# A decoder trunk on one core: the SBUF pools opened in another order

## The chip, the cores and the metric

The kernel runs on one NeuronCore of a Trainium2 chip. The metric is the device time of one execution in microseconds (us). The engines are TensorE (PE in the profile, its weight loads PEld), VectorE (DVE), ScalarE (ACT), GpSimd (POOL) and SyncE (SP), which here issues nearly all transfers.

## The reference, cut to what matters

Two layers of a decoder trunk on 256 tokens of width 1024, float32, with three parallel mixers, a cross-attention into 256 memory tokens and a gated feed-forward:

```python
for l in range(DEPTH):                                   # DEPTH = 2
    h = rmsnorm(x, norm_mix[l])
    p = h @ w_in[l]                                      # 1024 -> 5888 columns
    a_x, a_c, a_b, q, k, v, g, z, gates = jnp.split(p, IN_SPLITS, axis=-1)
    y_a = short_conv_mixer(a_x, a_c, a_b, conv_w[l]) @ w_a_out[l]
    r = retention(rotary(q), rotary(k), v, ret_gn[l])
    y_b = (jax.nn.silu(g) * r) @ w_b_out[l]
    y_c = spatial_gating(jax.nn.gelu(z), sg_ln[l], sg_w[l], sg_b[l]) @ w_c_out[l]
    g_a, g_b, g_c = jnp.split(jax.nn.sigmoid(gates), 3, axis=-1)
    x = x + (g_a * y_a + g_b * y_b + g_c * y_c) @ w_o[l]
    h = rmsnorm(x, norm_xa[l]); mm = rmsnorm(mem, norm_mem[l])
    x = x + cross_attention(h, mm, xa_q[l], xa_k[l], xa_v[l], xa_o[l])
    h = rmsnorm(x, norm_ffn[l])
    x = x + (jax.nn.silu(h @ w1[l]) * (h @ w3[l])) @ w2[l]
return rmsnorm(x, final_norm)
```

## The kernel before, in words

**Weights.** All weight matrices lie in HBM as one stream in the order of use, in 320 tiles of 128 partitions x 1024 float32 (512 KB each). `fetch` (lines 92 to 109) loads the next tile into one of 5 `raw` buffers through SP's queue, ACT rounds it into one of 4 `hi` buffers (line 106), and DVE subtracts to give the rest in one of 4 `lo` buffers (recorded under line 67, the helper `tt`). `hi` and `lo` have the type float32r. `weights` (line 111) fetches one tile ahead of the matmuls.

**Activations** are kept as such a pair too: `xs` is the normed residual (split at lines 201 and 202), `mo`, `mg`, `qx`, `pt`, `ox` (tag "op"), `mmt` (tag "M"), `kT` and the first half of the feed-forward's hidden layer `aA` (tag "A"), `vt` and the second half `aB` (tag "B").

**Products.** Every product is the sum of three: high by high, high by rest, rest by high. All TensorE instructions are recorded under line 43, where `InOrder` issues them in the order of the code. There are three kinds of stream:

- `chunk_T` (f, gt, ax, ac, ab, q, k, wo, xo, w): for each half i of a chunk a pair of matmuls, one of 512 moving columns (both parts of the activation) on the `hi` weights, then one of 256 moving columns on the `lo` weights. Here a weight tile is the stationary operand, the activation the moving one.
- `chunk_N` and `chunk_pair` (qk, v, z, g, the first xv): the weight tile moves, 512 columns at a time, and the activation is stationary.
- `chunk_y`, the scores s, the weighted values av, the narrow xv and the last two chunks of w: 256 moving columns in every matmul.

**Order.** TensorE's order is that of the code. A scheduler in the building library sets the order of the other engines. SP's loads of a `raw` buffer wait until DVE has read what was in it before.

**Memory.** A pool takes its place in SBUF when it is opened: `const`, `res` (`xT`, `xs`), `wts` (`raw`, `hi`, `lo`), `wrk` (all else), from low addresses to high. Each partition holds the same layout. PSUM pools (`psm`, `pss`) are apart.

Of the kernel before, what the change touches and what calls it, by code (L numbers as in the profile page):

```python
# [54 lines left out]
def decoder_trunk(ctx: ExitStack, tc: tile.TileContext, a, out):  # L55
    nc = tc.nc
    V, A, G, T = nc.vector, nc.scalar, nc.gpsimd, InOrder(tc, nc.tensor)

    const = ctx.enter_context(tc.tile_pool(name="const", bufs=1))
    res = ctx.enter_context(tc.tile_pool(name="res", bufs=1))  # L60
    wts = ctx.enter_context(tc.tile_pool(name="wts", bufs=3))
    wrk = ctx.enter_context(tc.tile_pool(name="wrk", bufs=2))
    psm = ctx.enter_context(tc.tile_pool(name="psm", bufs=2, space=bass.MemoryType.PSUM))
    pss = ctx.enter_context(tc.tile_pool(name="pss", bufs=4, space=bass.MemoryType.PSUM))

# [665 lines left out]
```

## Time and profile before

| | |
|---|---|
| device time, median of 3 runs | 968.31 us (968.21 to 970.08) |
| the profiled execution, its own time | 969.4 us |
| its span, first to last instruction | 967.6 us, mean granted clock 0.995 |
| PE busy | 951.8 us, 98% of the span |
| DVE, ACT, POOL busy | 713.7, 539.8, 296.1 us |
| transfers | 175.53 MB, 181 GB/s mean |

The span is the time between the first and the last instruction of the trace. The chain of work that ended last is followed back from the last instruction, at each step to what released it; its pieces name an engine, the tile that is written and the number of instructions. From a piece of one stream its start-to-start spacing follows as length over count. The duration of one matmul in the trace is longer than that spacing, since matmuls are pipelined.

### The profile page before, as it was taken

To read this page: it belongs to the slowest core of one execution; us is meant where nothing else is said; L and a number is where in the kernel's file an instruction comes from. 1 tells how busy PE (TensorE), PEld (TensorE's weight loads), DVE (VectorE), ACT (ScalarE), POOL (GpSimd) and SP (SyncE) were. 2 spreads that over 40 slices of the span, in tenths; PEclk is the share of its full clock that TensorE was granted. 3 is DMA by queue.
4 is the path that set the end of the run, shared out by engine and by line. 5 is a ranking of instruction groups with operands and counts; after the bars stand their busy time and mean duration, and the time that the engine had idled before them with its cause. 6 is when DMAs were issued, how large, how long until landed. Compare 5 with 4: busy or idle time off the path is not lost.

```text
span 967.6 us, 14606 instructions
## 1 busy us (share of the span) xinstructions
PE 951.8 (98%) x5622; PEld 836.8 (86%) x5622; DVE 713.7 (74%) x884; ACT 539.8 (56%) x740; POOL 296.1 (31%) x232
## 2 busy tenths in 40 slices
PE   8999999999999999999999989999999999999996
PEld 6788889888998888888888878998889888888886
DVE  7679789886768866657655896799776778666654
ACT  6565765565645755654456465545665466656431
POOL 5943021320114644432134230024100345444211
PEclk9999999999999999999999999999999999999998
DMA  9664665555546565555656355555644556556541
GB/s 310 245 228 145 192 203 186 190 182 170 172 133 194 177 198 191 193 187 180 197 179 194 111 180 193 195 179 172 196 153 151 154 187 191 187 194 194 180 151 44
DMA packets 52630, 175.53 MB, mean 181 GB/s; under 512 B 6096, under 2 KB 6608, under 8 KB 52560
## 3 DMA queue, kind: packets, MB, share of 16 engines
q1 hardware_dynamic: 52128, 174.03, 55.9%
q8 instruction: 44, 0.72, 0.3%
q10 hardware_dynamic: 432, 0.57, 0.2%
q14 instruction: 26, 0.21, 0.1%
HBM read 173.53 MB, written 1.05 MB: 180 GB/s over the span
## 4 chain that ended last, share of the span: by engine, by line
PE 96%; DVE 2%; DMA 1%; issue 0%; SPq 0%; ACT 0%; DVEq 0%
PE f L43 25%; PE gt L43 14%; PE w L43 13%; PE y L43 5%; PE k L43 5%; PE xo L43 5%; PE wo L43 5%; PE xv L43 5%; PE q L43 5%; PE z L43 2%; PE g L43 2%; PE v L43 2%; PE qk L43 2%; PE av L43 1%; PE ac L43 1%; PE s L43 1%
## 5 line engine op out<-in xcount | busy, mean ns | idle before, releaser
L67 DVE TENSOR_TENSOR lo<-raw,hi 128x1024 fp32r<-128x1024 f32 (+1 forms) x321 | 436.8, 1363 | 200.0 <-ACT hi L106 198.0
L106 ACT ACTIVATE hi<-raw 128x1024 fp32r<-128x1024 f32 (+1 forms) x321 | 338.9, 1057 | 315.1 <-issue 67.5
L43 PE MATMUL f<-xs,hi 128*128 128x512 f32 x704 | 245.2, 393 | 0.0
L43 PE MATMUL f<-xs,lo 128*128 128x256 f32 x704 | 196.1, 279 | 0.0
L43 PEld LDWEIGHTS f<-xs,hi 128*128 128x128 f32 x704 | 131.9, 187 | 30.1 <-issue 0.4
L43 PE MATMUL gt<-xs,hi 128*128 128x512 f32 x384 | 136.5, 400 | 2.8 <-DVE ev L67 2.7
L43 PEld LDWEIGHTS f<-xs,lo 128*128 128x128 f32 x704 | 132.6, 188 | 0.0
L67 POOL TENSOR_TENSOR sq<-xT 128x512 f32<-128x512 f32 x27 | 45.8, 1695 | 239.3 <-DVE xT L67 234.5
L43 PE MATMUL gt<-xs,lo 128*128 128x256 f32 x384 | 107.8, 281 | 0.0
L67 POOL TENSOR_TENSOR ev<-ev,rb_ffn 128x512 f32<-128x512 f32 x44 | 63.8, 1453 | 108.3 <-DVE ev L67 85.3
L43 PEld LDWEIGHTS gt<-xs,hi 128*128 128x128 f32 x384 | 72.7, 189 | 20.6 <-DVE ev L67 4.0
L43 PEld LDWEIGHTS gt<-xs,lo 128*128 128x128 f32 x384 | 73.2, 191 | 0.0
L43 PE MATMUL w<-aB,hi 128*128 128x512 f32 (+1 forms) x198 | 62.7, 372 | 0.0
L43 PE MATMUL w<-aA,hi 128*128 128x512 f32 (+1 forms) x198 | 62.3, 371 | 0.0
L67 POOL TENSOR_TENSOR ev<-ev 128x256 f32<-128x256 f32 x44 | 50.5, 1151 | 20.1 <-ACT ev L597 20.1
L202 DVE SCALAR_TENSOR_TENSOR xs<-xT,par,xs 128x256 fp32r<-128x256 f32 x48 | 49.1, 1062 | 4.2 <-ACT xs L201 4.2
L43 PE MATMUL w<-aB,lo 128*128 128x256 f32 x176 | 49.5, 281 | 0.0
L43 PE MATMUL w<-aA,lo 128*128 128x256 f32 x176 | 49.4, 281 | 0.0
L43 PE MATMUL y<-mo,hi 128*128 128x256 f32 x256 | 46.1, 283 | 0.0
L43 PE MATMUL k<-mmt,hi 128*128 128x512 f32 x128 | 45.6, 400 | 0.0
L43 PE MATMUL q<-xs,hi 128*128 128x512 f32 x128 | 45.5, 398 | 0.0
L43 PE MATMUL xo<-ox,hi 128*128 128x512 f32 x128 | 45.4, 399 | 0.0
(251 smaller groups left out, 1779.9 us busy)
## 6 DMA issues: line engine op xcount, KB each, us to landing
raw<-in_ws SPq DMA_DIRECT2D x304, 512.0 KB, 3.5
raw<-in_ws SPq DMA_DIRECT2D x32, 256.0 KB, 4.0
m<-in_memT SPq DMA_DIRECT2D x12, 256.0 KB, 4.0
xT<-in_xT SPq DMA_DIRECT2D x4, 256.0 KB, 5.2
dec<-in_dec SPq DMA_DIRECT2D x1, 512.0 KB, 6.0
wm<-in_wsT SPq DMA_DIRECT2D x2, 256.0 KB, 4.8
out<-xT ACTq DMA_DIRECT2D x2, 256.0 KB, 2.3
sgg<-in_sgg SPq DMA_DIRECT2D x1, 256.0 KB, 5.1
```

The source lines that it names most:

```text
L43: ins = getattr(self.engine, name)(*args, **kwargs)
L67: e.tensor_tensor(o, x, y, op=op)
L106: A.activation(hi[:, sl], raw[:, sl], AF.Copy)
L202: V.scalar_tensor_tensor(lo, x, scale, f32(hi), ALU.mult, ALU.subtract)
```

## The change

The two pools `wrk` and `wts` are opened ahead of `const` and `res`. Since the first pool that is opened gets the lowest addresses, everything moves:

```diff
+    wrk = ctx.enter_context(tc.tile_pool(name="wrk", bufs=2))
+    wts = ctx.enter_context(tc.tile_pool(name="wts", bufs=3))
     const = ctx.enter_context(tc.tile_pool(name="const", bufs=1))
     res = ctx.enter_context(tc.tile_pool(name="res", bufs=1))
-    wts = ctx.enter_context(tc.tile_pool(name="wts", bufs=3))
-    wrk = ctx.enter_context(tc.tile_pool(name="wrk", bufs=2))
     psm = ctx.enter_context(tc.tile_pool(name="psm", bufs=2, space=bass.MemoryType.PSUM))
```

Every engine's instructions stand in the same order with the same waits in both programs: 5024 rows on PE, 817 on DVE, 727 on ACT, 209 on POOL, 362 on SP. What differs is where the tiles lie. In bytes from the start of a partition, as the two built programs have them, with the remainder of the start by 256 behind it:

| tiles | before | after |
|---|---|---|
| `xs` | 34880 (64) | 211264 (64) |
| `xT` | 26688 (64) | 203072 (64) |
| `raw`, 5 buffers | 51264 to 71744 (64) | 139648 to 160128 (128) |
| `hi`, 4 buffers | 71744 to 88128 (64) | 160128 to 176512 (128) |
| `lo`, 4 buffers | 88128 to 104512 (64) | 176512 to 192896 (128) |
| tag "B": `aB`, `vt`, mixb | 110656 (64) | 22656 (128) |
| tag "M": `mmt`, mixm | 133184 (64) | 45184 (128) |
| tag "op", 2 buffers | 149568, 165952 (64) | 61568, 77952 (128) |
| tag "A": `aA`, `kT`, gs | 198656 (0) | 110656 (64) |
| `ev`, 4 buffers | from 187808 (160) | from 99808 (224) |
| m2 and pp, 2 buffers | from 223232 (0) | from 135232 (64) |

The matmul operands start at these addresses plus multiples of 512 bytes.

## Rows read from the trace of the kernel before

**Rows 1.** The page: busy time by engine, then the chain's shares.
```profile
PE 951.8 (98%) x5622; PEld 836.8 (86%) x5622; DVE 713.7 (74%) x884; ACT 539.8 (56%) x740; POOL 296.1 (31%) x232
PE 96%; DVE 2%; DMA 1%; issue 0%; SPq 0%; ACT 0%; DVEq 0%
```

**Rows 2.** Pieces of the chain: start us, us, engine, tile, count.
```profile
44.05 10.89 PE g L43 x48
91.22 22.19 PE gt L43 x128
119.63 27.73 PE gt L43 x160
147.36 23.03 PE y L43 x192
176.04 22.62 PE wo L43 x128
216.07 14.13 PE q L43 x80
231.61 5.55 PE q L43 x32
258.32 2.88 PE xv L43 x24
314.41 105.39 PE f L43 x608
419.81 62.10 PE w L43 x352
790.38 105.39 PE f L43 x608
```

**Rows 3.** Matmuls by form: tiles, shapes, count | busy us, mean ns | idle before.
```profile
L43 PE MATMUL f<-xs,hi 128*128 128x512 f32 x704 | 245.2, 393 | 0.0
L43 PE MATMUL w<-aB,hi 128*128 128x512 f32 x154 | 54.7, 398 | 0.0
L43 PE MATMUL w<-aA,hi 128*128 128x512 f32 x154 | 54.6, 397 | 0.0
L43 PE MATMUL q<-xs,hi 128*128 128x512 f32 x128 | 45.5, 398 | 0.0
L43 PE MATMUL g<-hi,xs 128*128 128x512 f32 x64 | 19.7, 389 | 0.0
```

**Rows 4.** One tile's matmuls: duration ns min/median/max, first and last start us, forms.
```profile
L43 PE MATMUL y<-mo,hi x256: 278/283/283, 147.2 to 646.1; 128*128 128x256 f32 x128
L43 PE MATMUL av<-pt,vt x96: 280/283/283, 261.0 to 752.8; 128*128 128x256 f32 x96
L43 PE MATMUL w<-aB,hi x12: 283/283/283, 947.9 to 949.8; 128*128 128x256 f32 x12
L43 PE MATMUL w<-aA,hi x11: 276/276/276, 951.7 to 953.4; 128*128 128x256 f32 x11
L43 PE MATMUL s<-kT,qx x96: 276/281/283, 230.0 to 726.4; 128*128 128x256 f32 x96
```

**Rows 5.** ACT's and DVE's work on the weight tiles, in the columns of rows 4.
```profile
L106 ACT ACTIVATE hi<-raw x321: 614/1061/1079, 5.5 to 946.5; 128x1024 fp32r<-128x1024 f32 x160, 128x512 fp32r<-128x512 f32 x1
L67 DVE TENSOR_TENSOR lo<-raw,hi x321: 679/1226/2361, 6.6 to 948.2; 128x1024 fp32r<-128x1024 f32 x160, 128x512 fp32r<-128x512 f32 x1
```

**Rows 6.** Transfers: SP's longest wait, then the loads of `raw` with their landing.
```profile
SPq L102 <- DVE lo L67: 745.5, 303, 8.1
raw<-in_ws SPq DMA_DIRECT2D x304, 512.0 KB, 3.5
```

**Rows 7.** PE's largest wait, then two stretches behind it (last three: PEclk, DMA share, GB/s).
```profile
PE gt L43 <- DVE ev L67: 2.7, 3, 2.1
577.00:580.00 3.00, 2.81 (x12) 2.37 (x13) 3.00 (x5) 1.77 (x3) 0.00 (x0) 0.74 0.71 203
580.00:584.00 4.00, 4.00 (x20) 3.48 (x19) 2.52 (x4) 1.58 (x2) 0.00 (x0) 0.77 0.73 252
```

## The prediction

> **What bounds the kernel now.** I read the page first: the busy times and the shares of the chain that ended last [rows 1]. PE is busy for 951.8 of 967.6 us and holds 96% of the chain; DVE with 2% and the transfers with 1% come in at the start and the end. So the time is the sum of the spacings of PE's matmuls, and the question is whether a spacing depends on where an operand lies. For that I read the chain's pieces one by one [rows 2] and divide length by count, since one piece is one stream without a break.
>
> The pairs of `chunk_T` (512 columns, then 256) show two spacings. f takes 105.39 us for 608 matmuls, which is 304 pairs at 346.7 ns; gt 22.19 us for 64 pairs and 27.73 us for 80, both 346.7 ns. But wo takes 22.62 us for 64 pairs, 353.4 ns; w 62.10 us for 176 pairs, 352.8 ns; q 14.13 us for 40 pairs, 353.2 ns, and right after that 5.55 us for 16 pairs, 346.9 ns. I call them the fast and the slow spacing; they lie 6.7 ns or 1.9% apart. 768 columns at one per cycle of the granted 2.4 GHz would be 320 ns. The streams of 256 columns alone have 23.03 us for 192 (y) and 2.88 us for 24 (xv), both 120.0 ns, and g with 512 columns alone 10.89 us for 48, 226.9 ns.
>
> Two things are to be seen in this. First, q reads the same `xs` at the same addresses in both its pieces and yet stands at either spacing: within the layout of before, a stream can hold both, and which one seems to be set by how it was entered. Second, one place shows the operand's address itself. The 256-column matmuls of w take 283 ns each on `aB` and 276 ns on `aA`, and s on `kT`, in the same place as `aA`, has 276 at least and 281 at the median, while y and av stay at 283 [rows 4]. A duration of 283 ns goes with a spacing of 120 (y), so 163 ns less: 281 is a spacing of 118, 276 one of 113. `aA` and `kT` are the only matmul operands that start at a multiple of 256 bytes; all others, weights included, start 64 bytes behind one.
>
> **The change part by part.** No instruction, wait or queue position moves, so nothing is added and nothing taken away; what can change is the length of what is there. The sum is made against the profiled execution (969.4 us, span 967.6, 1.8 us around it); its own time is 1.1 us over the median of 968.31, which is the base here.
>
> *ACT, DVE and the helpers.* ACT's rounding of a weight tile runs over all 20 combinations of 5 `raw` and 4 `hi` buffers, spread over 36 KB, and takes 1061 ns at the median and 1079 at most; DVE's subtraction has 1226 ns at the median, with cases up to 2361 [rows 5]. Taken: 0 us. If these did get longer, the cover is a wait: the engines are busy for 540 and 714 us of the span [rows 1], and only one place shows PE waiting for them for long, 2.1 us in gt of layer 1 [rows 7]. Behind that wait, in which PE stood still, the granted clock is 0.74 and 0.77 on the mean of two stretches of 3 and 4 us, a part of them at 1.2 GHz: 0.78 and 0.92 us lost. Both bounds of this item come from that place: it may go (-2.1 - 1.7 = -3.8 us) or appear in layer 0 as well (+3.8 us). The nearest row is the steady 1061, so 0.
>
> *Transfers.* SP waits for 745.5 us in total for `raw` buffers to come free, and a load lands 3.5 us after its issue [rows 6]. Loads stand ahead of need; a few tenths of a us more on each would be covered. 0 us.
>
> *Streams on `xs` (f, gt, ax, ac, ab, q).* 704 + 384 + 96 + 128 = 1312 pairs. `xs` keeps its start of 64 behind a multiple of 256; the weights go from 64 to 128. Bounds: all that is slow becomes fast, or all that is fast becomes slow. About 1000 of them are fast: the 704 of f, by their mean of 393 ns against 398 for q [rows 3], 144 of gt in layer 0 [rows 2] with an estimated 130 in layer 1, and 16 or more of q; some 300 are slow. So the ends are -300 x 6.7 ns = -2.0 us and +1000 x 6.7 ns = +6.7 us. I take 0, since the moving operand, whose start shows in rows 4, keeps its remainder.
>
> *Pairs on other operands (k, wo, xo, w).* 3 x 128 + 308 = 692 pairs, slow by wo and w [rows 2], on `aA` with remainder 0 and on `aB` with 64 alike [rows 3]. They can only stay or get fast: 0 to -4.6 us. Two remainders with one spacing: 0.
>
> *Streams of 256 columns.* y 384, av 96, the narrow xv 192: 672 matmuls at 120 ns, whose moving operand goes from remainder 64 to 128. Like the best of `aA` (113 ns) they would give 672 x 7 ns = -4.7 us, like its other value (118) -1.3 us, like themselves 0. No row shows 128. It is not a multiple of 256 either, so I count it with 64: 0. In return `aA` and `kT` lose their place: 96 of s and 66 of w by 2 to 7 ns, +0.3 to +1.1 us; taken +0.3.
>
> *Streams of 512 columns with moving weights (qk, v, z, g, wide xv):* 480 at 226.9 ns. The nearest row with another start is the 512-column matmul on `aA`, 397 ns against 389 for g [rows 3]: +8 x 480 = +3.8 us at one end; at the other they lose all over 512 cycles (213.3 ns), -6.5 us. Taken 0.
>
> Sum: 968.31 + 0.3, rounded to 968.5 us.
>
> A rule to set beside rows 2: the Trainium skill, "TensorE: Matmul & The Clock Gate", in the part on the step "56ns, not 53.3ns", gives a warm matmul its columns at 2.4 GHz and a fixed 2.5 ns, whatever the operands' place. By that a pair would take 325 ns, not 346.7 or 353.4, and this change would be worth exactly 0 with no chance left for anything else; the trace here doesn't agree, for it has two spacings for one shape.
>
> **The rivals.**
>
> *Slower: equal remainders were what made the fast spacing.* In all fast pairs now, moving operand and weights both start 64 behind a multiple of 128. The one place where they differ, `aA` (0) with `hi` (64), is slow in all seven chunks of w, also right after f, which was fast until then: the piece of w starts at 419.81, where f's ends [rows 2]. After the change `xs` (64) and `hi` (0 by 128) differ too. It decides as soon as what counts is the distance of the two operands rather than each start; then f and gt go slow, +6.7 us: 975.0 us. Against it: k, wo, xo have equal remainders now and are slow.
>
> *Faster: it is the remainder by 128 that counts.* Then `op`, `mmt`, `aB` and moving weights get what `aA` has now. y, av and xv gain 1.3 to 4.7 us, and the wide streams lie anywhere between +3.8 and -6.5. With 4.7 of the first and 0.2 of the second: 968.5 - 4.9 = 963.6 us. For it: y's 120.0 ns are 288 cycles and g's 226.9 are 544, each 32 more than its columns, as if a run of bytes that starts off a boundary cost a piece more. Against it: the pairs on `aA` show no gain at all.
>
> *The entry is drawn anew.* If the spacing hangs on the moment of entry alone, small shifts may turn whole stages: f of one layer slow is 320 x 6.7 ns = +2.1 us (970.6); k, wo, xo and q of both layers fast, some 480 pairs, -3.2 us (965.3).
>
> **How the numbers follow.** Within 0.2% (966.4 to 970.2, about what a measurement of this kernel can tell from no change): 0.40, the forecast and the small draws. The slower rival 0.28, a stage drawn slow 0.04: slower 0.32. The faster rival 0.24, stages drawn fast or the gt wait gone 0.04: faster 0.28. The forecast's own range is 966.4 to 970.2; since both signs hold 0.60, the range of 8 in 10 goes into both rivals: 963.0 to 975.5.
>
> **What would show it.** Right: the pieces of f, y and g in the chain keep 346.7, 120.0 and 226.9 ns. The slower rival: f's piece from 314 us on at 107.4 us instead of 105.39, gt slow throughout. The faster one: y under 23.03 us, av and y at 281 or 276 ns. If `hi<-raw` leaves 1061 ns, or PE waits for `hi` or `lo` in the middle of the program, I was wrong about the other engines.

## The result, and the profile after

The changed kernel takes 976.18 us (median of 4 runs, 975.23 to 977.01), the kernel before 969.19 beside it (4 runs, 968.21 to 972.3). The ratio is 1.0069, with a 95% interval of 1.0053 to 1.0084 (intervals stand in brackets from here on): slower by 7.0 us, where 968.5 was forecast and 975.5 was the end of the range. The profiled execution took 975.23 us with a span of 973.4, 5.8 more than before.

The page of the changed kernel: busy time by engine, then the two steps on the weight tiles and f's 512-column matmul (busy us, mean ns), and the loads of `raw`:

```profile
PE 959.2 (99%) x5622; PEld 839.6 (86%) x5622; DVE 710.9 (73%) x884; ACT 539.9 (55%) x740; POOL 296.5 (30%) x232
...
L67 DVE TENSOR_TENSOR lo<-raw,hi 128x1024 fp32r<-128x1024 f32 (+1 forms) x321 | 433.8, 1353 | 208.1 <-ACT hi L106 206.1
L106 ACT ACTIVATE hi<-raw 128x1024 fp32r<-128x1024 f32 (+1 forms) x321 | 339.0, 1057 | 324.5 <-issue 72.1
L43 PE MATMUL f<-xs,hi 128*128 128x512 f32 x704 | 249.5, 398 | 0.0
...
raw<-in_ws SPq DMA_DIRECT2D x304, 512.0 KB, 3.5
```

Against [rows 1] PE has 7.4 us more for the same 5622 matmuls and PEld 2.8 more; DVE, ACT and POOL have at most 0.4 more. The mean duration of f's 512-column matmul is 398 ns, which was q's value, instead of 393 [rows 3]. `raw` lands 3.5 us after its issue as in [rows 6].

Pieces of the chain of the changed kernel (start us, us, engine, tile, count), to be held against [rows 2]:

```profile
44.31 10.99 PE g L43 x48
...
91.68 22.61 PE gt L43 x128
...
120.61 28.27 PE gt L43 x160
148.88 23.03 PE y L43 x192
...
177.56 22.62 PE wo L43 x128
...
217.59 14.13 PE q L43 x80
233.13 5.65 PE q L43 x32
...
316.19 107.42 PE f L43 x608
423.60 62.11 PE w L43 x352
...
581.35 45.49 PE gt L43 x256
...
794.15 107.42 PE f L43 x608
```

f's 304 pairs take 353.4 ns each in both layers, where they took 346.7; gt's 64 and 80 pairs take 353.3 and 353.4. What was slow stays as it was (wo 22.62, w 62.11, q 14.13), and so does y at 120.0 ns. g goes from 226.9 to 229.0.

Taken from the start of one piece to the start of a later one, the 5.8 us lie here:

| stretch | change, us |
|---|---|
| f's two long pieces | +2.01, +2.03 |
| start, then z to the end of gt, layer 0 | +0.19, +1.33 |
| y to the long piece of f, both layers | +0.26, +0.36 |
| w of layer 0 to z of layer 1; from there to gt's long piece | +0.11, +0.26 |
| gt's long piece, layer 1 | -0.75 |
| last w to the end | 0.00 |

The one gain has its own reason. PE's largest wait in the changed kernel (us in total, times, longest):

```profile
PE gt L43 <- DVE ev L67: 2.5, 3, 2.1
```

and two stretches behind it (last three columns: granted clock, DMA share, GB/s):

```profile
581.00:584.00 3.00, 2.65 (x15) 2.33 (x16) 3.00 (x4) 1.94 (x3) 0.00 (x0) 1.00 0.79 220
584.00:588.00 4.00, 4.00 (x24) 3.49 (x23) 2.69 (x4) 2.46 (x3) 0.00 (x0) 1.00 0.81 256
```

The longest wait is 2.1 us as before [rows 7], but the granted clock behind it is 1.00, so 2.4 GHz throughout, where it was 0.74 and 0.77 [rows 7]. Before, the piece took 46.24 us, 1.86 more than 128 pairs at 346.7 ns; now 45.49, only 0.25 more than 128 pairs at 353.4. The pairs themselves cost 0.86 us more there, and 1.61 us of lost clock did not occur in this execution. It need not be an effect of the change: the first experiment has the changed kernel's distances, and its profiled execution lost the clock at this place.

### The profile page after: what moved, and what is told of

Same layout as the page of the kernel before. It is cut to its first block, busy times and chain, and to the rows that moved or that the text cites. A ratio compares the mean times of both kernels' runs of the same rounds, so it can differ in the third digit from the quotient of the medians.

```text
span 973.4 us, 14606 instructions
## 1 busy us (share of the span) xinstructions
PE 959.2 (99%) x5622; PEld 839.6 (86%) x5622; DVE 710.9 (73%) x884; ACT 539.9 (55%) x740; POOL 296.5 (30%) x232
## 3 DMA queue, kind: packets, MB, share of 16 engines
HBM read 173.53 MB, written 1.05 MB: 179 GB/s over the span
## 4 chain that ended last, share of the span: by engine, by line
PE 96%; DVE 2%; DMA 2%; issue 0%; ACT 0%; DVEq 0%; SPq 0%
PE f L43 26%; PE gt L43 14%; PE w L43 13%; PE y L43 5%; PE k L43 5%; PE xo L43 5%; PE wo L43 5%; PE q L43 5%; PE xv L43 5%; PE z L43 2%; PE g L43 2%; PE v L43 2%; PE qk L43 2%; PE av L43 1%; PE ac L43 1%; PE ab L43 1%
## 5 line engine op out<-in xcount | busy, mean ns | idle before, releaser
L43 PE MATMUL f<-xs,hi 128*128 128x512 f32 x704 | 249.5, 398 | 0.0
```

Of the source, the lines that this page charges most:

```text
L43: ins = getattr(self.engine, name)(*args, **kwargs)
```

## The experiments

The theory from here on is that of the slower rival: a spacing depends on the **distance** of a matmul's two operands, the start of the moving one less the start of the stationary one, by its remainder modulo 256 bytes. A *wide* matmul has 512 moving columns, a *narrow* one 256; a *pair* is one of each. These are the distances, in bytes:

| stream | before | after |
|---|---|---|
| pairs on `xs` (f, gt, q, ...) | 0 | -64 |
| pairs on `op`, `mmt`, `aB`; y, av, narrow xv | 0 | 0 |
| w on `aA`, s on `kT` | -64 | -64 |
| z, g, qk, v (weight tile moves) | 0 | +64 |

In the variants of the kernel only addresses differ, except where a diff shows more. `pad` stands for one unused tile ahead of a pool, as in the first diff; the diffs are cut to the lines that matter.

**Weights alone, by 64 bytes.** The kernel before, with everything from `raw` upward 64 bytes higher and `xs` in its place.

```diff
+    ctx.enter_context(tc.tile_pool(name="pad", bufs=1)).tile([P, 16], F32, name="pad")
     wts = ctx.enter_context(tc.tile_pool(name="wts", bufs=3))
```

> The kernel before, in its own order of pools, with 64 unused bytes ahead of the weight tiles: raw, hi, lo and the working pool move up by 64, xs stays where it was. Distance theory: f and gt go to 353.3 ns a pair for good, z and g to 228.9 ns, 976 us as the kernel after. Start theory: xs starts as before, so f and gt stay at 346.7 ns; 968 to 970 us. Place theory: nothing has changed its region or order, 968 to 970 us.

Measured: 976.11 us (975.48 to 976.98), ratio 1.0057 [1.0041, 1.0073]. The chain of this kernel:

```profile
44.45 11.00 PE g L43 x48
...
91.80 22.60 PE gt L43 x128
...
316.31 107.42 PE f L43 x608
...
581.50 47.00 PE gt L43 x256
...
795.79 107.42 PE f L43 x608
```

The pieces of the changed kernel, in the old order of the pools. 64 bytes of padding do what the change did. Only gt's long piece in layer 1 differs, 47.00 us where the changed kernel's profile had 45.49, and behind the wait ahead of it the clock was low again (third column from the end):

```profile
581.00:584.00 3.00, 2.50 (x11) 2.19 (x12) 3.00 (x4) 2.08 (x4) 0.00 (x0) 0.80 0.68 216
584.00:588.00 4.00, 4.00 (x18) 3.38 (x18) 2.73 (x4) 1.58 (x2) 0.00 (x0) 0.72 0.74 251
```

With the clock lost in both profiles, the spans are 7.2 us apart (974.8 and 967.6).

**The distance put back in the changed kernel.** 64 bytes ahead of `const`, after the weights: `xs` gets the weights' remainder.

```diff
     wts = ctx.enter_context(tc.tile_pool(name="wts", bufs=3))
+    pad, 64 bytes
     const = ctx.enter_context(tc.tile_pool(name="const", bufs=1))
```

> The kernel after, with 64 unused bytes between the weight tiles and the constants: only the constants, xT and xs move, so that xs and the hi and lo tiles start at the same remainder by 128 again (both 0). Distance theory (what counts is the difference of the moving operand's start and the weights' start by 128): f and gt return to about 346.7 ns a pair, z and g to 226.9 ns, 969 to 970 us. Start theory (the moving operand's own start by 128 counts): xs now starts at 0, a remainder it had in neither kernel, so a spacing of neither or the slow one, 974 to 977. Place theory (the region or order of the pools counts): 64 bytes change nothing, 976 us.

Measured: 970.39 us (968.06 to 972.94, 10 runs) against 970.34 for the kernel before beside it (19 runs), ratio 0.9998 [0.9985, 1.0011]. The loss is gone with the pools still in the new order and the weights still at remainder 128, so it was not the weights' own start. But the chain of its profiled execution has one f slow and one fast:

```profile
91.78 22.19 PE gt L43 x128
...
315.06 107.42 PE f L43 x608
...
792.91 105.39 PE f L43 x608
```

**Everything by 64 bytes, all distances kept, in the kernel before.** This tells the distance from each start alone, on which my forecast rested.

```diff
+    pad, 64 bytes
     const = ctx.enter_context(tc.tile_pool(name="const", bufs=1))
```

> The kernel before with 64 unused bytes ahead of everything: each operand moves by 64, all distances stay. Distance theory: 968 to 970 us, each stream's spacing as before (y 120.0 ns, aA 113 to 118). Start theory: y, av and the narrow xv, which now start at a multiple of 128, go to 113 to 118 ns (1.3 to 4.7 us faster), aA to 120. Place theory: 968 to 970 us.

Measured: 971.93 us (969.63 to 973.47, 10 runs), ratio 1.0011 [0.9995, 1.0027]: no change beside the 970.34 of the kernel before, though above the 968 to 970 expected. y stays at 120.0 ns although all its operands have new remainders, and gt stays fast; both f were slow in the profiled execution:

```profile
119.72 27.73 PE gt L43 x160
147.46 23.03 PE y L43 x192
...
314.61 107.42 PE f L43 x608
...
792.68 107.42 PE f L43 x608
```

So at distance 0 f can take either value, 2.03 us apart, and one execution can hold both (layers 0 and 1 of the run before this one). At distance -64 I saw only the slow one.

**Streams alone, by distance.** A program that holds nothing but such streams, executed once: 32 pairs, 32 matmuls of 256 columns, 24 of 512, for each of 18 combinations of starts.

```python
x = mov[:, m + 512 * (k % 4):m + 512 * (k % 4) + 512]      # m, w: the two offsets, in elements of 4 bytes
T.matmul(ps[:, i].rearrange("p t s -> p (t s)"), wgt[:, c:c + P], x, ...)            # c = w + multiples of 128
T.matmul(ps[:, i, 1], wgt[:, c:c + P], x[:, 0:S], ...)
```

> Only streams of matmuls on two operands in SBUF, none of the trunk: for each of 18 pairs of starts (moving operand from 0 to 192 bytes behind a multiple of 256 against weights at a multiple of 256, and five pairs with both moved) one piece of 32 pairs of 512 and 256 columns, one of 32 matmuls of 256 columns and one of 24 of 512, with two one-column matmuls ahead of each. The output is the input x, so no product is kept. Distance theory: distance 0 gives 346.7 or 353.3 ns a pair, 120 ns and 226.7 ns, distance 64 gives 353.3, 113 to 118 and 228.9, and (64, 64) is as (0, 0), (0, 64) as (64, 0), distance 128 as 0; between them (16, 32, 96) unknown, by steps of 32 or in proportion. Start theory: (64, 64) is as (64, 0) and (0, 64) as (0, 0). Place theory: all starts alike.

Start-to-start spacing in ns, first four matmuls left out (moving offset / weights' offset in bytes):

| | 0/0 | 4/0 | 16/0 | 32/0 | 64/0 | 64/64 | 0/64 | 0/32 |
|---|---|---|---|---|---|---|---|---|
| pair | left out: first stream, 425 on the mean | 360.2 | 346.7 | 346.7 | 353.5 | 346.5 | 353.1 | 353.1 |
| 256 columns | 119.8 | | | 116.7 | 117.7 | | 113.3 | |
| 512 columns | 227 | | 231.3 | 233.3 | 228.9 | | | |

One shape, and from 346.5 to 360.2 ns. Each stream was entered once, so where a spacing also hangs on the entry (next program) the table has one of its values. The +64 of the wide streams gives 228.9 ns: g's 229.0 of the changed kernel. Two guesses on record failed here. The sign counts: 0/64 is not as 64/0 (wide 233.5 against 228.9; narrow 113.3 against 117.7, though 0/64 gave 117.8 in the next program). And the period is not 128: 128/0 and 0/128 gave 350.9 and 350.8 ns a pair, a value that distance 0 never took, while 192/0, the same distance as 0/64 modulo 256, agreed with it in all three (352.8, 113.3 and 233.5).

**What sets the spacing at one distance.** Each stream of 16 pairs is entered ten times, after `gap(n)`, which is 1 to 8 matmuls of one column, and straight after a narrow and a wide stream.

```python
for n in range(1, 9):
    gap(n); mixed("mix" + letter + chr(96 + n), m, w, 8)
alike("nar" + letter, m, w, 256);    mixed("mix" + letter + "y", m, w, 8)
alike("wid" + letter, m, w, 512, 24); mixed("mix" + letter + "z", m, w, 8)
```

> Streams of matmuls alone, none of the trunk; the output is the input x, no product is kept. For eight pairs of starts (moving, weights, in bytes behind a multiple of 256: 0/0, 64/64, 0/64, 64/0, 32/0, 96/64, 64/32, 16/0) a piece of 16 pairs of 512 and 256 columns is entered from a run of 1 to 8 one-column matmuls, from a stream of 256 columns and from one of 512. Entry theory: at distance 0 (0/0 and 64/64) some entries give 346.7 ns a pair and others 353.3, and the spacing then stays for the piece; at 64 (0/64, 64/0) every entry gives 353.3. If the spacing at distance 0 hangs on the place instead, all entries of 0/0 agree with each other, and all of 64/64. Distance 32 (32/0, 96/64, 64/32): 346.7 from every entry if the 346.7 of the piece at 32/0 was its rule, both values if it was its entry.

The chain of this program; the letter behind `mix` is the pair of offsets (a 0/0, c 0/64, d 64/0, e 32/0), the last one the entry. The trace records each matmul of `gap` as two:

```profile
25.78 0.34 PE gap L43 x4
26.12 5.66 PE mixab L43 x32
31.78 0.56 PE gap L43 x6
32.34 5.76 PE mixac L43 x32
...
72.95 3.84 PE nara L43 x32
76.79 5.65 PE mixay L43 x32
...
173.38 5.76 PE mixcb L43 x32
...
241.13 5.69 PE mixda L43 x32
...
247.16 5.76 PE mixdb L43 x32
...
320.69 5.67 PE mixeb L43 x32
...
326.92 5.66 PE mixec L43 x32
```

`mixab` and `mixac` are the same stream at distance 0, 5.66 and 5.76 us: one matmul of one column more ahead of it (x6 instead of x4) cost some 6.6 ns on each pair that follows. An entry behind such matmuls takes some 0.1 us itself; straight after a narrow stream (`mixay`) there is none, and 5.65 us is 353.1 ns a pair, slow. Behind one-column matmuls distance 0 held both spacings (at 0/0 two of eight entries fast, the first of the eight being the program's first stream, at 407 ns; at 64/64 three of eight); straight after a stream it was slow each time. Distance -64 held only the slow one (352.6 to 353.4), and distance +32 only the fast one (346.6 to 347.6 in all entries, at 32/0, 64/32 and 96/64). Distance 0 is not alone in having a choice: 64/0, expected slow from every entry, gave 348.7 to 349.1 ns from four entries and 352.9 to 353.5 from six, and 16/0, at 346.7 in the table, went up to 360.0. So +32 is the distance for a better layout.

**Distance +32 for every activation that moves over weights.** The kernel before with 224 bytes ahead of `wts`, 32 ahead of `wrk` and 64 ahead of tag "A".

```diff
+    pad, 224 bytes
     wts = ctx.enter_context(tc.tile_pool(name="wts", bufs=3))
+    pad, 32 bytes
     wrk = ctx.enter_context(tc.tile_pool(name="wrk", bufs=2))
...
+        wrk.tile([P, 16], F32, tag="pad", name="pada", bufs=1)
         gs = wrk.tile([P, 24, S], F32, tag="A", name=f"gs{l}", bufs=1)
```

> The kernel before, with unused bytes ahead of the weight tiles (224), of the working pool (32) and of tag A (64), so that every moving activation starts 32 bytes behind its weights by 256, in all streams of pairs. If distance 32 is fast from every entry: all 2004 pairs at 346.7 ns, of which some 1000 are slow in the kernel before, -6.7 us; the streams of 512 columns with moving weights at -32 go from 226.9 to up to 233.3 ns, 480 x 6.4 = +3.1 us; the 256-column ones on y 384 x -3 = -1.2 us: 965 us beside a kernel before of 970. If distance 32 has two spacings as distance 0 has: between 965 and 977. If only 0 and 64 differ and 32 counts as 64: 976.

Measured: 965.48 us (963.99 to 966.56, 5 runs), ratio 0.9956 [0.994, 0.9971] beside 969.52. Its chain:

```profile
45.07 11.20 PE g L43 x48
...
120.79 27.75 PE gt L43 x160
148.53 22.40 PE y L43 x192
...
176.48 22.19 PE wo L43 x128
...
313.73 105.40 PE f L43 x608
419.13 61.03 PE w L43 x352
```

wo and w are fast now (346.7 ns a pair), y gains 3.3 ns a matmul, and the wide streams lose: g 233.3 ns at distance -32.

**The same distances in the changed kernel.** Pads of 64, 160 and 96 bytes ahead of tag "A", `wts` and `const`: the new order of the pools, the distances of the last run.

> The kernel after, in its order of pools, with unused bytes ahead of tag A (64), the weight tiles (160) and the constants (96), so that all moving activations start 32 bytes behind their weights by 256. Distance theory: as the kernel before at distance 32, 965 to 966 us, all pairs at 346.7 ns. Place theory, if a part of the 7 us hung on where the pools lie: between 966 and 976.

Measured: 964.57 us (963.64 to 965.67, 4 runs), ratio 0.9934 [0.9909, 0.9959]. Both f at 105.40, y at 22.40, g at 11.20. The order of the pools by itself costs nothing that shows here.

**The wide streams back at 0 as well.** Tiles whose columns move start 8 elements further into a slightly longer buffer.

```diff
-        hi = wts.tile([P, TW], F32R, tag="hi", name=f"hi{n}", bufs=4)
+        at = 8 if n % 160 < 16 or 78 <= n % 160 < 82 else 0
+        hi = wts.tile([P, TW + 64], F32R, tag="hi", name=f"hi{n}", bufs=4)[:, at:at + TW]   # lo alike
-            rb = wrk.tile([P, S], F32, tag="rb", name=name, bufs=2)
+            rb = wrk.tile([P, S], F32, tag="rb", name=name, bufs=1)                         # for room
```

> The kernel of distance 32, in which hi and lo tiles are 256 bytes longer and those that move in the 512-column streams (qk, v, z, g, wide xv) are written and read 32 bytes further in, so that these streams stand at distance 0 and all pairs stay at 32 (one small buffer less makes room). Distance theory: the wide streams go from up to 233.3 back to 226.7 ns, 480 x 6.6 = 3.2 us less, pairs stay at 346.7: 962 to 963 us where the kernel at distance 32 has 965.5. If the wide streams were slower for another reason than their distance: 965.5.

Measured: 963.84 us (963.0 to 964.16, 6 runs), ratio 0.9926 [0.9904, 0.9947] beside 970.65. In its chain g is back, the rest stays:

```profile
44.25 10.88 PE g L43 x48
...
119.63 27.75 PE gt L43 x160
147.37 22.40 PE y L43 x192
```

This version has the lowest time of all, just above the 962 to 963 expected, and is faster than both kernels; its interval overlaps with that of the run before, so the 0.7 us between those two are not shown by the times. The chain shows g back at 226.7 ns, which is the step that was tried.

**Finer steps, and where the theory stops.** Two more programs of streams alone, each executed once, went over the distances, one in steps of 4 to 16 bytes with three entries each, one in all steps of 4 bytes from 0 to 252 with two entries each, the weights at 0 in both.

```python
mixed("mix" + letter + entry, m, 0, 6)      # m: 0 to 63 elements of 4 bytes
```

> Streams of matmuls alone, none of the trunk; the output is the input x, no product is kept. Weights at a multiple of 256 bytes, the moving operand 0 to 240 bytes behind one, in steps of 16 and some finer round 32; at each three pieces of 12 pairs entered from 2, 3 and 5 one-column matmuls, then 20 matmuls of 256 columns and 14 of 512. Distance theory: one map with a period of 256 bytes, 0 with two spacings, 32 with one (346.7), 192 (= -64) with 353.3, 224 (= -32) with about 353 and 118 ns in narrow, 233.3 in wide streams, as at 0/32. If the spacing goes by the distance in proportion, values between 32 and 64 lie between 346.7 and 353; if by lines of some size, in steps.

> Streams of matmuls alone, none of the trunk; the output is the input x, no product is kept. Weights at a multiple of 256 bytes, the moving operand at each distance from 0 to 252 bytes in steps of 4; at each two pieces of 12 pairs (entered from 2 and 5 one-column matmuls), 12 matmuls of 256 columns and 10 of 512. Distance theory, by the pieces so far: 343.6 ns a pair at 28 from both entries, 346.7 at 32, 36 at 346.7 to 355.6, and no distance under 340. If the pieces so far hung on their entry instead, 28 and 32 change here.

The pairs lie between 343 ns (28, 60 and 236 bytes) and 360. 36 bytes, expected at 346.7 to 355.6, gave 357.2 and 358.7 in the second. The chain of the second (`ab` 4 bytes, `ah` 28, `ai` 32; 12 pairs each):

```profile
34.53 4.42 PE mixabb L43 x24
...
117.37 4.23 PE mixahb L43 x24
...
130.86 4.28 PE mixaib L43 x24
```

By distance alone 28 bytes had to beat 32 in the kernel, so I took the last version with every stationary tile 4 bytes further in:

```diff
-        at = 8 if n % 160 < 16 or 78 <= n % 160 < 82 else 0
+        at = 8 if n % 160 < 16 or 78 <= n % 160 < 82 else 1
```

> The kernel with wide streams at distance 0, whose pair streams read hi and lo 4 bytes further in, so that moving operands start 28 bytes behind their weights. Distance theory with the 343.6 ns of the stream at 28: 2004 pairs x 3.1 = 6.2 us less, y 384 x 1.0 = 0.4 us less: 957 to 958 us where distance 32 has 963.8. If the lengths of ACT's and DVE's work on tiles that start 4 bytes off a multiple of 32 grow and come onto the path, or the 343.6 was the entry's: 962 to 966.

Measured: 970.9 us (969.16 to 971.79, 11 runs), ratio 1.0004 [0.9994, 1.0013], the time of the kernel before: a miss by some 13 us. Its chain:

```profile
91.87 22.40 PE gt L43 x128
...
148.54 23.04 PE y L43 x192
...
315.10 106.40 PE f L43 x608
```

350.0 ns a pair, where the stream alone had 343.6 at 28/0. Here the starts are 64 and 36. The other engines are not the cause: ACT's rounding takes 1063 ns at the median where the last version had 1061, DVE's subtraction 1227 and 1226, and 2004 pairs at 3.3 ns with y's 0.64 us a layer make up 7.9 of the 8.1 us between the two spans. So in steps finer than 32 bytes the distance is not the whole rule, and the starts themselves count. Where all starts were multiples of 32 bytes, equal distances gave the pairs the same set of spacings to within some 1 ns, in the cases tried (0/0 and 64/64; 32/0, 64/32 and 96/64; 0/64 and 192/0; 0/32 and 224/0).

## Why the prediction was wrong, point by point

**The step that failed** is the term "Streams on `xs`": taken 0, "since the moving operand, whose start shows in rows 4, keeps its remainder". It gave the effect to the start of one operand. Moving the weights alone by 64 bytes cost what the whole change cost; moving both cost nothing in gt or y; padding `xs` back took the loss away. What counts is the distance of the two, and the change made it -64 for every pair on `xs`. The term measured +6.85 us in the profile, the upper bound that I had put at +6.7.

**The rival that came true** named this mechanism and its point of decision, with 6.7 us. The measured 7.0 us is near it, and the profile adds it up: long pieces of f 4.06 and its shorter ones 0.29, gt 1.05 in layer 0 and 0.86 in layer 1 (46.24 and 45.49 us less the lost clock), ax, ab and q 0.59, together 6.85 us. With 0.34 for z and g, 0.23 at the start and in xv, and 1.61 us of clock not lost in this execution, the spans' 5.8 us are accounted for. I gave it 0.28 and ended the range 0.5 us above its price of 975.0. Of the 1.2 us by which 976.18 lies above that price, 0.9 is the base: the kernel before measured 969.19 beside the changed one, not 968.31.

**The argument I held against it** was that k, wo and xo have equal remainders and are slow. That is true but doesn't speak against it. Distance 0 does not make a pair fast, it leaves it two spacings; k follows straight on y and wo on k, xo on av, and at distance 0 a stream entered straight after a narrow one was slow both times that was tried (`mixay` and the same at 64/64). That this is why they are slow is a guess that fits. q's two spacings in [rows 2] already said that equal distance allows both. The sign I should have weighed more was w on `aA`, slow right after a fast f: the one stream of pairs at another distance in the trace, and it had only the slow value.

**The rule of the Trainium skill** ("TensorE: Matmul & The Clock Gate", step "56ns, not 53.3ns") names the columns and the clock and no address; taken as valid at any address, as the prediction took it, it would have made this change worth 0. The measurement decides against that for these float32r pairs: 7.0 us from addresses alone.

**Terms that held.** Nothing for pairs on `op`, `mmt` and `aB`: wo 22.62 us both times. Nothing for the 256-column streams y, av and xv: y 23.03. Nothing for ACT, DVE and the transfers: 1061 ns at the median for `hi` in both profiles, 3.5 us to landing. q's slow piece, which was at the slow value already, keeps its 14.13 us.

**Terms that were off in size.** Streams with moving weights: taken 0, measured +0.34 us in z and g (229.0 instead of 226.9 ns; the bound of +3.8 came from a matmul of another kind). `aA` and `kT`: taken +0.3, measured 0.0 (w 62.10 and 62.11). They did move off their multiple of 256 bytes, but that start was not what made them short; they kept their distance of -64, and s keeps its 281 ns at the median. The rival by the remainder by 128 is out, since y did not move.

**The draw of entries** was priced right, 2.1 us for one f: 2.03 in the profiles. In the kernel I saw it at distance 0 alone (the streams alone also had a choice at 64/0 and 16/0). The kernel before ran from 967.67 to 974.99 us over all its runs, and the last layout with its pairs at +32, where no draw was seen, from 963.0 to 964.16; that the draws are all of that unevenness is not shown.

**Open.** The profile has no view that tells why a distance changes the spacing, and nothing here shows it. What in an entry decides between the two spacings at distance 0 is open too, as is the rule below 32 bytes. And why the clock fell behind gt's wait in the profiles of the kernel before and of the first experiment (47.00 us) and not in that of the changed kernel, after waits of 2.1 us in all three, was not tried.

## What to carry to other kernels

Where TensorE is the bound, divide the length of each unbroken piece of the chain by its count: two values for one shape are a cost that the busy shares do not show. Tabulate both operands' start addresses, and their distance, before judging a change that "only moves memory"; then a tile or two of padding is an edit to try, here worth 0.4 to 0.7%. A layout that admits two spacings can also make measurements uneven (each f drawn slow costs 2.03 us here), so a change can look faster or slower by what its entries happen to draw.

## What was not expected of the hardware

- Start-to-start of 512 and 256 columns in float32r, at 2.4 GHz and with no wait: 343 to 360 ns, by operand addresses and, at some distances, by the entry. The two shapes in themselves want different distances: in the kernel and in the streams alone 256 columns took 120.0 ns at 0 and 116.7 at +32, 512 columns 226.7 at 0, 228.9 at +64 and 233.3 at +-32.
- At distance 0 a stream holds one of two spacings from its entry on, for 304 pairs in f (105.39 or 107.42 us).
- 4 bytes can matter: 353.5 ns at 64/0, 343.2 at 60/0; and 346.7 against 350.0 in the kernel when the weights moved from 32 to 36.
